# The mixer's output projection in seven block products, in an fp32 encoder kernel on one Trainium2 core

## The chip, the cores and the metric

The kernel runs on one core of one Trainium2 chip. The metric is the device time of one execution in microseconds (us), as the median of three runs.

## The reference

A trunk of two layers over x of 512 tokens by 1024 channels, in float32. Each layer is a half-step SwiGLU FFN, a token mixer, and another half-step FFN; one RMSNorm ends it. What the change touches is the last line of the mixer.

```python
def token_mixer(h, w_in, ..., w_out, lam_init):
    proj = h @ w_in
    ...
    gates = jax.nn.sigmoid(...)
    merged = gates[:, :, 0] * y_pool + gates[:, :, 1] * y_attn + gates[:, :, 2] * y_lru
    return merged @ w_out            # (512 x 1024) @ (1024 x 1024)

def reference(x, ...):
    for l in range(DEPTH):           # 2
        x = x + 0.5 * swiglu(rms_norm(x, ffn1_norm[l]), ffn1_w_in[l], ffn1_w_out[l])
        x = x + token_mixer(rms_norm(x, mix_norm[l]), ...)
        x = x + 0.5 * swiglu(rms_norm(x, ffn2_norm[l]), ffn2_w_in[l], ffn2_w_out[l])
    return rms_norm(x, final_norm)
```

## The kernel before

**Precision.** Every large matmul is done as three: each fp32 operand is split into a high part (a copy to a rounded type, on ScalarE, ACT) and a low part (operand minus high part, on VectorE, DVE), and hi·hi + hi·lo + lo·hi go into the same accumulator. For weights the parts are named `wh` and `wl`, for the merged activations `mg` (both parts), for the FFN's input `zh` and `zl`.

**Units.** The work is a list of units. A unit is a weight block of 128x1024 in SBUF (512 KB, tile `raw`, loaded by SyncE's queue, SP), its split, and its matmuls (`mm`). The main loop records a unit's matmuls and then a "gap" (`gap`), in which the work that stands between two units is recorded: the evictions of the unit just done (`after`), tasks that were deferred by so many gaps (`defer`), and the splits of the units up to `look` ahead (3 as a rule, up to 7 around a change of stage). Each engine then works through its own instructions in that order.

**Seven products.** The FFNs' two projections already use Strassen-Winograd's form (`seven`): rows and columns of the product and the contraction are each halved, and seven block products P1, P2, Q5, Q3, P6, P7, Q4 stand in for eight. Their left operands are blocks A11, A12, A22 of the activations or sums of them (S1 to S4). Their right operands are sums of weight blocks, and these are made by DMA: a block is loaded into `raw`, and when it has been split, GpSimd (POOL) issues a second DMA that accumulates the next block into the same tile. The results are added into the residual `x` (eight tiles of 128x512) by DVE, a product at a time (`put`, `total`); a product that is used more than once is first copied out of PSUM by ACT (tile `u`).

**The mixer's end.** Four units `y1` multiply the attention output by its branch weights, each for a pair of column chunks. After each, DVE merges the branches into tiles `gt` and splits them into `mg` (six ops of 128x512). Then the output projection: for each of two column halves four units of `w_out`, each with two contraction chunks for all four row tiles, into four PSUM banks `o`. At the end of a half DVE adds 0.5·`o` into `x`. Calls of `done` follow: ACT squares `x` for the norm, TensorE transposes it (`zt`), ACT evicts the transposes (`zf`), and `zh`, `zl` and sums `zs` are made for the FFN behind. In all but the last part of the projection the FFN's weights are split ahead.

Of the kernel before, what the change touches and what calls it, by code (L numbers as in the profile page):

```python
# [17 lines left out]
S = 512  # L18
# [89 lines left out]
def trunk_kernel(ctx, tc, xn, pm, fin, cst, bd, f1i, f1o, win, wbp, wba, wbl, wout, f2i, f2o, out):  # L108
# [72 lines left out]
    units = []  # L181
    hooks = {}
# [227 lines left out]
    LEFT = {"P1": "A11", "P2": "A12", "Q5": "S1", "Q3": "S4", "P6": "S2", "P7": "S3", "Q4": "A22"}  # L410

    def seven(order, nk, width, left, wap, after, held, prep=None, fresh=False):
# [6 lines left out]
        for p in order:  # L419
            name = LEFT[p]  # L420
            for n, (k0, k1) in enumerate(parts):
# [40 lines left out]
                units.append(Unit(block, flat((k1 - k0) * width), mm, fin, acc=acc, held=held[p] if isinstance(held, dict) else held, nk=k1 - k0))  # L462


    def ffn(wi, wo, done, order0, rf, lim0=12, wait=1):
# [176 lines left out]
        def prep(p, n, i):  # L642
            if n % 2 == 0:
                sums, parts = combos(LEFT[p], n // 2)
                if LEFT[p] in ("S1", "S4", "S3"):
                    add_hook(i - 4, sums)
                add_hook(i - 3, parts)
            else:
                add_hook(i, lambda k=(LEFT[p], n // 2): comb.pop(k))

        def put(hh, kk, src, sign=1.0):
            for tt in range(2):
                xv = x[2 * (hh ^ rf) + tt, kk]
                V.scalar_tensor_tensor(out=xv, in0=src[tt], scalar=0.25 * sign, in1=xv, op0=MUL, op1=ADD)

        def copies(dst):
            def fn(ps):
                dst.update(enumerate(two("u")))
                for tt in range(2):
                    A.activation(out=dst[tt], in_=ps[tt], func=AF.Copy)  # L660
            return fn

        def total(ps):
            for tt in range(2):
                V.tensor_tensor(out=u[tt], in0=ps[tt], in1=u[tt], op=ADD)

        def o_p1(ps):
            copies(u)(ps)
            later.append(lambda: put(0, 0, u))

        def o_p2(ps):
            later.append(lambda: put(0, 0, ps))
            defer(1, lambda: done(0 ^ rf, 0))

        def o_q5(ps):
            copies(q5)(ps)
            later.append(lambda: put(0, 1, q5))
            defer(1, lambda: later.append(lambda: put(1, 1, q5)))
            defer(2, q5.clear)

        def o_q3(ps):
            later.append(lambda: put(0, 1, ps))

        def o_p6(ps):
            later.append(lambda: (total(ps), put(0, 1, u, -1.0)))
            defer(1, lambda: done(0 ^ rf, 1))

        def o_p7(ps):
            later.append(lambda: (total(ps), put(1, 1, u, -1.0)))
            defer(1, lambda: (later.append(lambda: (put(1, 0, u), u.clear())), done(1 ^ rf, 1)))  # L690

        def o_q4(ps):
            put(1, 0, ps)
            done(1 ^ rf, 0)
# [5 lines left out]
        def left(name, k):  # L700
# [3 lines left out]
              {"P1": o_p1, "P2": o_p2, "Q5": o_q5, "Q3": o_q3, "P6": o_p6, "P7": o_p7, "Q4": o_q4},  # L704
# [3 lines left out]
    def mixer(l, side, done, between):  # L708
# [393 lines left out]
        def y1(cpair):  # L1102
# [83 lines left out]
        for ch in (1, 0):  # L1186
            box = {"held": []}
            for u4 in range(4):
                b = Block([load_fn(wout[l][u4 * 256:u4 * 256 + 256, ch * S:(ch + 1) * S].rearrange("(k p) f -> p k f", p=128), 2, S)])

                def part(ts, box):
                    for t in ts:
                        for k0, uh, ul in box["held"]:
                            for k in (k0, k0 + 1):
                                wh, wl = (a[:, (k - k0) * S:(k - k0 + 1) * S] for a in (uh, ul))
                                th, tl = (a[:, t * 128:(t + 1) * 128] for a in st["mg"][k])
                                PE.matmul(box["ps"][t], lhsT=th, rhs=wh, start=k == 0, stop=False)
                                PE.matmul(box["ps"][t], lhsT=th, rhs=wl, start=False, stop=False)
                                PE.matmul(box["ps"][t], lhsT=tl, rhs=wh, start=False, stop=k == KD - 1)

                def mm(u, a0, a1, u4=u4, ch=ch, box=box):
                    if u4 == 0:
                        box["ps"] = [bank("o") for _ in range(4)]
                    box["held"].append((2 * u4, u.hi, u.lo))
                    if ch == 0 and u4 >= 2:
                        if u4 == 3:
                            part((2, 3), box)
                        return
                    part(range(4), box)
                    box["held"].clear()  # L1210
# [409 lines left out]
```

## Time and profile before

| | |
|---|---|
| median of 3 runs | 2115.81 us (2114.51 to 2118.64) |
| the profiled execution's own time | 2117.74 us |
| its span, first to last instruction | 2115.9 us |
| mean granted TensorE clock | 0.997 |
| busy: TensorE / DVE / ACT / POOL | 2072.8 / 1658.6 / 1191.2 / 343.7 us |
| DMA | 314.61 MB, 149 GB/s |

Busy times are sums over the span. A matmul's row is longer than the distance to the next one, because matmuls are pipelined; what one costs is read from the starts of its neighbours. A number in square brackets behind an instruction in the timeline is the time for which its engine stood idle ahead of it, with what ended that. Almost every line reads L83, because a helper records the operations; the tile names tell them apart.

### The profile page before, as it was taken

How to read it: one execution, taken by the hardware profiler on the slowest of the kernel's cores; microseconds unless marked ns; L12 is line 12 of the kernel's file. 1: busy time of each engine (PE TensorE's matmuls, PEld its weight loads, DVE VectorE, ACT ScalarE, POOL GpSimd, SP SyncE). 2: the span in 40 equal slices, each digit the busy share in tenths (PEclk: the TensorE clock that was granted, in tenths of full speed). 3: DMA queues.
4: the chain of work that ended last, by engine and by line, in shares of the span. 5: the costliest groups of instructions: out<-in, count | busy, mean ns of one | idle time of the engine just before them, and what ended most of it. 6: DMA issues, size and time to landing. Idle time of an engine off the chain costs nothing.

```text
span 2115.9 us, 26228 instructions
## 1 busy us (share of the span) xinstructions
PE 2072.8 (98%) x9646; PEld 1734.1 (82%) x9646; DVE 1658.6 (78%) x2362; ACT 1191.2 (56%) x1766; POOL 343.7 (16%) x292
## 2 busy tenths in 40 slices
PE   8999999999999999999999999999999999999998
PEld 6988888788787889888879887887887877988786
DVE  6788898597677588779977878986967766788797
ACT  7555566645663565556755555665456536555564
POOL 1312230000000022213213222300000001322230
PEclk9999999999999999999999999999999999999999
DMA  9987997022226379889959879940221364887994
GB/s 252 180 184 159 210 193 216 1 79 90 70 80 189 80 148 193 162 203 196 228 104 205 172 157 239 183 154 20 84 82 54 117 180 79 163 192 164 205 179 102
DMA packets 194096, 314.61 MB, mean 149 GB/s; under 512 B 10544, under 2 KB 86832, under 8 KB 193968
## 3 DMA queue, kind: packets, MB, share of 16 engines
q0 software_dynamic: 76288, 138.43, 39.5%
q1 hardware_dynamic: 117392, 174.30, 24.8%
q8 instruction: 75, 1.23, 0.2%
q14 instruction: 53, 0.43, 0.1%
q10 hardware_dynamic: 288, 0.21, 0.0%
HBM read 310.80 MB, written 2.10 MB: 148 GB/s over the span
## 4 chain that ended last, share of the span: by engine, by line
PE 80%; DVE 9%; ACT 4%; DMA 4%; issue 2%; POOL 1%; DVEq 0%; SPq 0%; POOLq 0%; ACTq 0%
PE P L83 26%; PE Q L83 19%; PE ps L83 18%; PE o L83 4%; PE y L83 4%; DVE wl L83 4%; DMA raw<-in_f1i_dram 2%; PE v L83 2%; PE ht L83 2%; PE sc L83 1%; PE av L83 1%; ACT wh L83 1%; ACT zh L83 1%; DVE c L83 1%; DVE x L83 1%
## 5 line engine op out<-in xcount | busy, mean ns | idle before, releaser
L83 DVE TENSOR_TENSOR wl<-raw,wh 128x1024 fp32r<-128x1024 f32 (+2 forms) x696 | 705.7, 1038 | 163.4 <-ACT wh L83 153.7
L83 ACT ACTIVATE wh<-raw 128x1024 fp32r<-128x1024 f32 (+2 forms) x695 | 606.9, 906 | 208.2 <-DMA raw<-in_f2i_dram 53.0
L83 PE MATMUL ps<-z,wh 128*128 128x512 f32 x1216 | 380.1, 393 | 0.2
L372 POOL DMA_DIRECT2D raw<-in_f2i_dram x96 | 116.0, 1240 | 1114.4 <-DVE mg L83 353.2
L83 PE MATMUL P<-wl,zh 128*128 128x512 f32 (+1 forms) x768 | 287.3, 374 | 7.2 <-DVE wl L83 7.1
L83 PE MATMUL P<-wh,zh 128*128 128x512 f32 (+1 forms) x768 | 288.7, 376 | 4.7 <-ACT wh L83 3.1
L83 PE MATMUL P<-wh,zl 128*128 128x512 f32 (+1 forms) x768 | 286.5, 373 | 0.5 <-DVE zl L83 0.5
L83 PEld LDWEIGHTS ps<-z,wh 128*128 128x128 f32 x1216 | 227.1, 188 | 51.1 <-issue 3.4
L83 PE MATMUL ps<-z,wl 128*128 128x512 f32 x608 | 237.0, 390 | 0.0
L83 PE MATMUL Q<-wl,zh 128*128 128x512 f32 (+1 forms) x576 | 214.6, 373 | 6.1 <-DVE wl L83 6.1
L83 PE MATMUL Q<-wh,zh 128*128 128x512 f32 (+1 forms) x576 | 216.7, 376 | 2.1 <-ACT zh L83 1.9
L83 PE MATMUL Q<-wh,zl 128*128 128x512 f32 (+1 forms) x576 | 214.2, 372 | 1.0 <-DVE zl L83 1.0
L372 POOL DMA_DIRECT2D raw<-in_f1i_dram x96 | 116.1, 1236 | 366.9 <-DVE wl L83 274.2
L83 PEld LDWEIGHTS P<-wl,zh 128*128 128x128 f32 x768 | 145.1, 189 | 30.5 <-DVE wl L83 10.4
L83 PEld LDWEIGHTS P<-wh,zh 128*128 128x128 f32 x768 | 144.8, 189 | 25.7 <-ACT wh L83 3.5
L83 PEld LDWEIGHTS P<-wh,zl 128*128 128x128 f32 x768 | 145.0, 189 | 21.3 <-DVE zl L83 1.0
L83 PE MATMUL P<-wl,ah 128*128 128x512 f32 x352 | 138.1, 392 | 2.4 <-DVE wl L83 2.3
L83 PE MATMUL P<-wh,ah 128*128 128x512 f32 x352 | 137.5, 391 | 0.0
L83 PE MATMUL P<-wh,al 128*128 128x512 f32 x352 | 137.2, 390 | 0.0
L83 PEld LDWEIGHTS ps<-z,wl 128*128 128x128 f32 x608 | 114.1, 188 | 23.7
L83 PEld LDWEIGHTS Q<-wl,zh 128*128 128x128 f32 x576 | 108.2, 188 | 23.1 <-DVE wl L83 9.2
L83 PEld LDWEIGHTS Q<-wh,zh 128*128 128x128 f32 x576 | 108.2, 188 | 17.3 <-ACT zh L83 2.7
(192 smaller groups left out, 3414.4 us busy)
## 6 DMA issues: line engine op xcount, KB each, us to landing
raw<-in_win_dram SPq DMA_DIRECT2D x84, 512.0 KB, 4.7
raw<-in_f1i_dram POOLq DMA_DIRECT2D x64, 512.0 KB, 6.9
raw<-in_f2i_dram POOLq DMA_DIRECT2D x64, 512.0 KB, 6.9
raw<-in_f2i_dram SPq DMA_DIRECT2D x52, 512.0 KB, 5.5
raw<-in_f1i_dram SPq DMA_DIRECT2D x50, 512.0 KB, 6.2
raw<-in_f1o_dram POOLq DMA_DIRECT2D x40, 512.0 KB, 7.9
raw<-in_f2o_dram POOLq DMA_DIRECT2D x40, 512.0 KB, 8.3
raw<-in_f1o_dram SPq DMA_DIRECT2D x30, 512.0 KB, 7.5
```

The lines of the kernel that those rows point to most:

```text
L83: return fn(*args, **kw)
L372: return lambda raw: GP.dma_start(out=raw[:, 0:n * w].rearrange("p (k f) -> p k f", f=w), in_=src, accum_op=ADD)
```

## The change

The output projection of the mixer goes through `seven` as the FFNs do, in the order P1, P2, Q5, P7, P6, Q3, Q4, so that A11 and A12 come first. The merged tiles `gt` are kept (`st["mf"]`), sums S1 to S4 of them are made in DVE (`ms`), and split into `mh` and `ml`. What the FFN's output projection does with its results moves into a function, `added`, that both use. The start of the projection joins the list of places around which units are split further ahead (up to seven).

```diff
-    LEFT = {"P1": "A11", "P2": "A12", "Q5": "S1", "Q3": "S4", "P6": "S2", "P7": "S3", "Q4": "A22"}
+    SEVEN = {"P1": "A11", "P2": "A12", "Q5": "S1", "Q3": "S4", "P6": "S2", "P7": "S3", "Q4": "A22"}
...
                 elif p == "Q3":
                     block = b2[n] = Block([ld(1, 1)])
-                    acc = ap(0, 1)
+                    acc = ap(0, 1) if order.index("P7") > order.index("Q3") else None
+                elif order.index("P7") < order.index("Q3"):
+                    block = Block([ld(1, 1)], ap(0, 1))
...
+    def added(scale, rf, done, seventh=False):
...
+        def put(hh, kk, src, sign=1.0):
+            for tt in range(2):
+                xv = x[2 * (hh ^ rf) + tt, kk]
+                V.scalar_tensor_tensor(out=xv, in0=src[tt], scalar=scale * sign, in1=xv, op0=MUL, op1=ADD)
...
+        def p1(ps):
+            copies(u)(ps)
+            later.append(lambda: put(0, 0, u))
+            if seventh:
+                defer(1, lambda: later.append(lambda: put(0, 1, u, -1.0)))
+
+        def p2(ps):
+            later.append(lambda: put(0, 0, ps))
+            defer(1, lambda: done(0 ^ rf, 0))
+
+        def q5_(ps):
+            copies(q5)(ps)
+            later.append(lambda: put(0, 1, q5))
+            defer(1, lambda: later.append(lambda: put(1, 1, q5)))
+            defer(2, q5.clear)
+
+        def q3(ps):
+            if seventh:
+                put(0, 1, ps)
+                return done(0 ^ rf, 1)
...
+        def p6(ps):
+            if seventh:
+                later.append(lambda: (total(ps), put(1, 1, u, -1.0), put(0, 1, ps, -1.0)))
+                return close22()
...
+        def p7(ps):
+            if seventh:
+                return later.append(lambda: total(ps))
...
+        def close22():
+            defer(1, lambda: (later.append(lambda: (put(1, 0, u), u.clear())), done(1 ^ rf, 1)))
+
+        def q4(ps):
+            put(1, 0, ps)
+            done(1 ^ rf, 0)
...
+                if cpair == 3:
+                    defer(1, lambda: m_sum("S1"))
+                    defer(2, lambda: m_sum("S3"))
+                    defer(4, lambda: m_sum("S2"))
+                    defer(6, lambda: m_sum("S4"))
...
-        for ch in (1, 0):
-            box = {"held": []}
-            for u4 in range(4):
...
-                def part(ts, box):
...
+        def m_sum(name):
+            a, b, op = {"S1": ("A21", "A22", SUB), "S2": ("S1", "A11", SUB), "S3": ("A11", "A21", SUB), "S4": ("A12", "S2", ADD)}[name]
+            a, b = m_block(a), m_block(b)
+            t = sums[name] = big(name="ms")
+            for o, p, q in zip(m_block(name), a, b):
+                V.tensor_tensor(out=o, in0=p, in1=q, op=op)
+            hi, lo = big(F32R, "mh"), big(F32R, "ml")
+            A.activation(out=hi, in_=t, func=AF.Copy)
+            later.append(lambda: V.tensor_tensor(out=lo, in0=t, in1=f(hi), op=SUB))
+            mc[name] = (hi, lo)
...
+        results = added(0.5, rf, done, True)
+        changes.append(len(units))
...
+        seven(["P1", "P2", "Q5", "P7", "P6", "Q3", "Q4"], 4, S, left, wap, {p: then(p) for p in results}, 12)
...
-                units[i - 6 + k].look = look
+                units[i - 6 + k].look = max(look, units[i - 6 + k].look)
```

The next rows are DVE's in the changed kernel, in the middle of the projection of layer 0, from the row behind the low part of S1 to the second update of `x_116`. `x_114` and `x_116` are the tiles that the first transposes read, `ms_5813` is S1, `ms_5835` S3 and `ms_5887` S2; `u_5832` is the copy of P1's results, `P2_5860` a PSUM bank of P2, `gt` the merged tiles.

```order
L83 TENSOR_TENSOR ms_5835<-gt_3981 128x512
L83 TENSOR_TENSOR ms_5835<-gt_5066 128x512
L83 SCALAR_TENSOR_TENSOR x_114<-u_5832,x_114 128x512
L83 SCALAR_TENSOR_TENSOR x_116<-u_5832,x_116 128x512
L83 TENSOR_TENSOR ml_5839<-ms_5835,mh_5838 128x1024
L83 TENSOR_TENSOR wl_5842<-raw_5599,wh_5841 128x1024
L83 SCALAR_TENSOR_TENSOR x_118<-u_5832,x_118 128x512
L83 SCALAR_TENSOR_TENSOR x_120<-u_5832,x_120 128x512
L83 TENSOR_TENSOR ms_5887<-ms_5813,gt_3981 128x512
L83 TENSOR_TENSOR ms_5887<-ms_5813,gt_5066 128x512
L83 SCALAR_TENSOR_TENSOR x_114<-P2_5859,x_114 128x512
L83 SCALAR_TENSOR_TENSOR x_116<-P2_5860,x_116 128x512
```

In the kernel before DVE's rows at that place, from the last `mg` of layer 0 to the first half's evictions, are these.

```order
L83 TENSOR_TENSOR mg_5766<-gt_5540,mg_5766 128x512
L83 TENSOR_TENSOR wl_5769<-raw_5513,wh_5768 128x1024
L83 TENSOR_TENSOR wl_5806<-raw_5556,wh_5805 128x1024
L83 TENSOR_TENSOR wl_5843<-raw_5589,wh_5842 128x1024
L83 TENSOR_TENSOR wl_5873<-raw_5663,wh_5872 128x1024
L83 SCALAR_TENSOR_TENSOR x_118<-o_5779,x_118 128x512
L83 SCALAR_TENSOR_TENSOR x_120<-o_5780,x_120 128x512
L83 SCALAR_TENSOR_TENSOR x_98<-o_5777,x_98 128x512
L83 SCALAR_TENSOR_TENSOR x_100<-o_5778,x_100 128x512
```

Four splits and four evictions stood there; now twelve ops stand between S1's low part and the tiles that the first transposes read.

TensorE's rows at the place where these transposes now stand, between the last matmuls of Q5 and the first of P7 (`cst` holds the identity).

```order
L83 MATMUL Q5_5902<-wl_5750,mh_5816 128x512
L83 MATMUL Q5_5902<-wh_5749,ml_5817 128x512
L83 MATMUL zt_5942<-cst_71,x_114 128x128
L83 MATMUL zt_5942<-cst_71,x_116 128x128
L83 MATMUL zt_5942<-cst_71,x_114 128x128
L83 MATMUL zt_5942<-cst_71,x_116 128x128
L83 MATMUL zt_5949<-cst_71,x_114 128x128
L83 MATMUL zt_5949<-cst_71,x_116 128x128
L83 MATMUL zt_5949<-cst_71,x_114 128x128
L83 MATMUL zt_5949<-cst_71,x_116 128x128
L83 MATMUL P7_5964<-wh_5790,mh_5838 128x512
```

Before, the first transposes stood between matmuls of the second column half and read `x` tiles whose evictions were the last DVE work of the first half. Now they stand between two products, and the second of them reads the last row of the DVE piece above.

The third place is the transposes in the middle of Q4. On DVE, the last rows up to the tiles that they read are these in the changed kernel (`Q3_6056` and `Q3_6057` are Q3's banks, `raw_5711` and `raw_5796` already weights of the next FFN).

```order
L83 SCALAR_TENSOR_TENSOR x_118<-P6_6000,x_118 128x512
L83 SCALAR_TENSOR_TENSOR x_120<-P6_6001,x_120 128x512
L83 TENSOR_TENSOR wl_6039<-raw_5473,wh_6038 128x1024
L83 TENSOR_TENSOR wl_6042<-raw_5708,wh_6041 128x1024
L83 SCALAR_TENSOR_TENSOR x_106<-u_5832,x_106 128x512
L83 SCALAR_TENSOR_TENSOR x_108<-u_5832,x_108 128x512
L83 TENSOR_TENSOR wl_6076<-raw_5711,wh_6075 128x1024
L83 TENSOR_TENSOR wl_6079<-raw_5796,wh_6078 128x1024
L83 SCALAR_TENSOR_TENSOR x_118<-Q3_6056,x_118 128x512
L83 SCALAR_TENSOR_TENSOR x_120<-Q3_6057,x_120 128x512
```

The updates from Q3 stand behind three splits of the next FFN's weights. In the kernel before, at the end of its second half, DVE's rows ahead of the last evictions but two were these.

```order
L83 TENSOR_TENSOR wl_6020<-raw_5732,wh_6019 128x1024
L83 TENSOR_TENSOR wl_6023<-raw_5774,wh_6022 128x1024
L83 TENSOR_TENSOR wl_6032<-raw_5809,wh_6031 128x1024
L83 TENSOR_TENSOR wl_6035<-raw_5812,wh_6034 128x1024
L83 SCALAR_TENSOR_TENSOR x_114<-o_5930,x_114 128x512
L83 SCALAR_TENSOR_TENSOR x_116<-o_5931,x_116 128x512
```

What moved: the splits ahead of the next FFN stood there before too, but ahead of one addition to each `x` tile; now each tile is updated up to five times in the stage.

## Rows read from the trace of the kernel before

**Rows 1.** The page's first part: busy us, share of the span, instructions.

```profile
PE 2072.8 (98%) x9646; PEld 1734.1 (82%) x9646; DVE 1658.6 (78%) x2362; ACT 1191.2 (56%) x1766; POOL 343.7 (16%) x292
```

**Rows 2.** Waits of TensorE by releaser: us in total, times, longest.

```profile
PE P L83 <- DVE wl L83: 9.4, 10, 1.7
PE Q L83 <- DVE wl L83: 7.6, 12, 2.1
```

**Rows 3.** Timeline of TensorE, layer 0: start, us, instruction, count.

```profile
667.63 0.39 PE L83 MATMUL y<-at,wl 128*128 128x512 f32 x1
...
680.80 0.39 PE L83 MATMUL o<-wh,mg 128*128 128x512 f32 x1
...
681.26 0.61 PE L83 MATMUL o<-wh,mg 128*128 128x512 f32 x2
...
681.94 0.61 PE L83 MATMUL o<-wh,mg 128*128 128x512 f32 x2
```

**Rows 4.** Stretches of 20 us: busy us of each engine, clock, DMA share, GB/s.

```profile
660.00:680.00 20.00, 18.89 (x81) 14.71 (x80) 16.54 (x25) 6.74 (x10) 2.41 (x2) 1.00 0.65 175
680.00:700.00 20.00, 20.00 (x90) 16.57 (x89) 11.60 (x14) 6.64 (x8) 0.00 (x0) 1.00 0.63 185
700.00:720.00 20.00, 20.00 (x99) 16.78 (x98) 12.29 (x13) 13.28 (x24) 2.42 (x2) 1.00 0.16 43
720.00:740.00 20.00, 18.67 (x89) 14.99 (x88) 12.47 (x26) 12.04 (x25) 1.23 (x2) 1.00 0.53 98
```

**Rows 5.** Timeline of DVE, layer 0, the mixer's end.

```profile
666.55 0.69 DVE L83 TENSOR_TENSOR at<-o,at 128x512 fp32r<-128x512 f32 x1 [0.69 <-ACT at L83]
...
669.77 0.68 DVE L83 SCALAR_TENSOR_TENSOR gt<-gt,y 128x512 f32<-128x512 f32 x1
...
673.81 0.68 DVE L83 SCALAR_TENSOR_TENSOR gt<-gt,y 128x512 f32<-128x512 f32 x1
...
687.87 4.63 DVE L83 TENSOR_TENSOR wl<-raw,wh 128x1024 fp32r<-128x1024 f32 x4 [0.26 <-ACT wh L83]
...
702.76 1.89 DVE L83 SCALAR_TENSOR_TENSOR x<-o,x 128x512 f32<-128x512 f32 x3 [0.67 <-PE o L83]
...
720.85 0.69 DVE L83 SCALAR_TENSOR_TENSOR x<-o,x 128x512 f32<-128x512 f32 x1 [0.70 <-PE o L83]
```

**Rows 6.** Timeline of ACT, layer 0, the same place.

```profile
686.79 3.89 ACT L83 ACTIVATE wh<-raw 128x1024 fp32r<-128x1024 f32 x4
...
708.64 3.03 ACT L83 ACTIVATE zf<-zt,par 128x256 f32<-128x256 f32 x8 [1.30 <-PE zt L83]
...
722.73 0.20 ACT L83 ACTIVATE m<-m 128x2 f32<-128x2 f32 x1 [0.43 <-DVE m L83]
```

**Rows 7.** DMA issues from 640 to 800 us: count, KB, median us to landing.

```profile
raw<-in_f2i_dram POOLq DMA_DIRECT2D x8, 512.0 KB, 7.0
```

**Rows 8.** Timeline of TensorE at the FFN's Q5, layer 0 and layer 1.

```profile
734.32 0.50 PE L83 MATMUL Q<-wh,zh 128*128 128x512 f32 x1 [0.81 <-ACT zh L83]
...
735.58 0.50 PE L83 MATMUL Q<-wh,zl 128*128 128x512 f32 x1 [0.52 <-DVE zl L83]
...
1780.67 0.50 PE L83 MATMUL Q<-wh,zl 128*128 128x512 f32 x1 [0.53 <-DVE zl L83]
```

**Rows 9.** The page's part on DMA issues, the slowest group there.

```profile
raw<-in_f2o_dram POOLq DMA_DIRECT2D x40, 512.0 KB, 8.3
```

**Rows 10.** Timeline of TensorE between the layers.

```profile
1068.12 0.33 PE L83 MATMUL zt<-cst,x 128*128 128x128 f32 x1 [2.88 <-DVE x L83]
...
1080.39 0.54 PE L83 MATMUL P<-wh,zl 128*128 128x512 f32 x1 [0.53 <-DVE zl L83]
1080.73 0.63 PE L83 MATMUL P<-wh,zh 128*128 128x512 f32 x1
...
1084.14 0.39 PE L83 MATMUL P<-wh,zl 128*128 128x512 f32 x1
```

**Rows 11.** One stretch there, columns as in rows 4.

```profile
1082.00:1083.00 1.00, 1.00 (x4) 0.80 (x3) 0.61 (x1) 0.36 (x1) 0.97 (x1) 0.50 0.00 0
```

More of the change, by code (lines that the diff above doesn't have):

```diff
@@ L462, in seven, with copies, fn, total @@
                 units.append(Unit(block, flat((k1 - k0) * width), mm, fin, acc=acc, held=held[p] if isinstance(held, dict) else held, nk=k1 - k0))
+    def added(scale, rf, done, seventh=False):
+        u, q5 = {}, {}
+        def put(hh, kk, src, sign=1.0):
+            for tt in range(2):
+                xv = x[2 * (hh ^ rf) + tt, kk]
+                V.scalar_tensor_tensor(out=xv, in0=src[tt], scalar=scale * sign, in1=xv, op0=MUL, op1=ADD)
+        def copies(dst):
+            def fn(ps):
+                dst.update(enumerate(two("u")))
+                for tt in range(2):
+                    A.activation(out=dst[tt], in_=ps[tt], func=AF.Copy)
+            return fn
+        def total(ps):
+            for tt in range(2):
+                V.tensor_tensor(out=u[tt], in0=ps[tt], in1=u[tt], op=ADD)
+        def p1(ps):
[15 more added lines that the diff above has]
+                return done(0 ^ rf, 1)
+            later.append(lambda: put(0, 1, ps))
+        def p6(ps):
+            if seventh:
+                later.append(lambda: (total(ps), put(1, 1, u, -1.0), put(0, 1, ps, -1.0)))
+                return close22()
+            later.append(lambda: (total(ps), put(0, 1, u, -1.0)))
+            defer(1, lambda: done(0 ^ rf, 1))
+        def p7(ps):
+            if seventh:
+                return later.append(lambda: total(ps))
+            later.append(lambda: (total(ps), put(1, 1, u, -1.0)))
+            close22()
+        def close22():
[3 more added lines that the diff above has]
+            done(1 ^ rf, 0)
+        return {"P1": p1, "P2": p2, "Q5": q5_, "Q3": q3, "P6": p6, "P7": p7, "Q4": q4}
     def ffn(wi, wo, done, order0, rf, lim0=12, wait=1):
@@ L648, in prep @@
             else:
[L649 to L694, printed above, removed]
+                add_hook(i, lambda k=(SEVEN[p], n // 2): comb.pop(k))
+        results = added(0.25, rf, done)
         def wap(r, c, k0, k1):
@@ L1185, in mixer @@
         units[n0].between = between
-        for ch in (1, 0):
-            box = {"held": []}
-            for u4 in range(4):
-                b = Block([load_fn(wout[l][u4 * 256:u4 * 256 + 256, ch * S:(ch + 1) * S].rearrange("(k p) f -> p k f", p=128), 2, S)])
-                def part(ts, box):
[L1192 to L1210, printed above, removed]
-                def evict(hh, ch, box):
-                    for tt in range(2):
-                        t = 2 * hh + tt
-                        V.scalar_tensor_tensor(out=x[t, ch], in0=box["ps"][t], scalar=0.5, in1=x[t, ch], op0=MUL, op1=ADD)
-                    done(hh, ch)
-                def after(u4=u4, ch=ch, box=box):
-                    if u4 == 3:
-                        evict(1, ch, box)
-                        if ch == 1:
-                            evict(0, ch, box)
-                            box.clear()
-                units.append(Unit(b, flat(), mm, after, held=11))
@@ L1227, in last_mm, with m_block @@
-        def last_mm(u, a0, a1, box=box):
-            part((0, 1), box)
-            box["held"].clear()
-            st["mg"] = None
-        def last_after(box=box):
-            evict(0, 0, box)
-            box.clear()
-        units.append(Unit(None, [], last_mm, last_after, held=11))
+        rf = 1
+        sums = {}
+        def m_block(name):
+            if name in sums:
+                return [sums[name][:, j * S:(j + 1) * S].rearrange("p (c q) -> p c q", c=2) for j in range(2)]
+            r, k = (int(name[1]) - 1) ^ rf, int(name[2]) - 1
+            return [t.rearrange("p (c q) -> p c q", c=2)[:, :, r * 256:r * 256 + 256] for j in range(2) for t in (st["mf"][2 * k + j],)]
```

38 lines of the change are left out of this document (31 added, 7 removed).

## The prediction

> **What bounds the kernel now.** I read the page's first part first: TensorE is busy for 98% of the span, VectorE (DVE) for 78%, ScalarE (ACT) for 56% [rows 1]. Time follows TensorE, and the question for an edit is how much matmul it removes and how many waits it adds. The list of TensorE's waits comes next: 17 us for weight splits `wl` in the whole kernel [rows 2]. Then the stage itself: in the output projection of layer 0 the 128x512 matmuls follow each other without a gap, three of them (hi·hi, hi·lo, lo·hi) in 681.94 - 681.26 = 0.68 us (two start in the first of these rows, one between them), so 0.2267 us each; the stage starts at 680.80 [rows 3]. Last I read DVE in stretches of 20 us from 660 to 740: 16.5, 11.6, 12.3 and 12.5 us busy [rows 4], so it has 27 us free in these 80, most of it inside the projection. That free time is what the change spends.
>
> **What the change removes.** Eight block products (two row halves, two column halves, two halves of the contraction) become seven. One is 2 row tiles x 4 chunks x 3 = 24 matmuls, so there are 48 fewer in the two layers: 5.44 us a layer at 0.2267 us, 10.9 us in all, if TensorE stays gapless.
>
> **What it adds.** Per layer DVE gets six more weight splits `wl` (14 units in place of 8) and four low parts `ml`, ten ops of 128x1024; and eight adds `ms` and 24 updates and totals in place of 8 evictions, 24 more ops of 128x512. A `wl` follows the one ahead of it after 1.13 us (four in 4.63 us, the last 1.23 us long); a 512 op follows an independent one after 0.60 us (three in 1.89 us), and one on which it depends after 0.72 us [rows 5]. I take 1.135 and 0.63. That makes 10 x 1.135 + 24 x 0.63 = 26.5 us more DVE work, against 5.44 us less on TensorE. The 27 us free above would just hold it if each could be used where it stands.
>
> It can't. From P1 to Q4 a product takes TensorE 5.44 us, and DVE on average 2.57 ops of 1024 and 4.57 of 512, 5.8 us; and DVE enters the stage with the merges of the last two column pairs still to do. The stage turns from TensorE's into DVE's. ACT gets six `wh`, four `mh` and four copies, some 12 us, and has more than that free [rows 4], but each stands between two DVE ops. SP issues six loads in place of eight, GpSimd eight accumulating DMAs; DMA is busy for 0.63 of the time in the first 20 us of the stage and 0.16 in the second [rows 4], so I cost the bytes at nothing, and only the landing of one accumulate below.
>
> **The walk**, in the clock of the trace of before, layer 0. DVE is free after the last attention low part, at 667.24 [rows 5]; the first merge tile is complete on TensorE at 667.63 + 0.39 = 668.02 [rows 3]. The merge of one pair of column chunks takes DVE 673.81 - 669.77 = 4.04 us [rows 5]. In the new order two pairs come first (to 676.1), then four `wl`, the last behind ACT's fourth copy (0.95 us apart, four in 3.89 us [rows 6]), to 681.0, then the third pair to 685.1. TensorE reaches P1 at 680.80 as before and finds all it needs.
>
> Next on ACT is the copy for the second half of Q5, whose weights are an accumulating DMA that can be issued when `wl` of P1's second half ends, at 677.7. The nearest row for its landing is 7.0 us [rows 7]: about 685. Behind that copy stand, on ACT and DVE, the fourth pair's `mg`. So `wl` ends near 687.4 and the fourth pair at 691.5; P2's second half wants it from 689, and TensorE waits some 1.5 us. Then come `wl`, the two adds of S1, ACT's `mh` (1.05 us) and `ml`, at 696.55: Q5 waits 2.1 us for `mh` and 0.8 for `ml`, and ends at 701.6 in place of 697.1. From 696.5 DVE has ten 512 ops and two of 1024 before `x` is complete for the first transposes, 10 x 0.63 + 2 x 1.135 = 8.6 us: 705.1. **TensorE waits 3.5 us there.**
>
> P7, P6, Q3 and half of Q4 (84 matmuls) with 16 transposes run on to 725.8. DVE has 18 ops of 512 and 11 of 1024 in that stretch, 11.3 + 12.5 us, and 1.4 us of holes while ACT is held by evictions of the transposes (eight in 3.03 us [rows 6]): the two updates from Q3 end at 730.3, and the transposes that need them stand in the middle of Q4. **TensorE waits 4.5 us.** After the rest of Q4 (733.8) the next FFN's first matmul needs its `zh`. From an update's end to the end of ACT's small root it took 722.93 - 721.54 = 1.4 us [rows 5, 6]; four evictions, two `wh` and the `zh` follow on ACT, 1.5 + 1.9 + 1.05 us: 736.1, a wait of 2.3 us, and `zl` holds it 1.1 us more. The next transposes wait 1.0 us for `x`, and the third matmul of the FFN's Q5, which needs `zl` of S1, comes at 745.7. In the trace of before it comes at 735.58, after waits of 0.81 and 0.52 us [rows 8]. Layer 0 ends up **10.1 us late**: 16.8 us of waits, less the 1.3 that stood there, less the 5.4 saved. From there DVE has the work of before and some four units of split weights in hand, so I let the delay stay and not grow.
>
> Layer 1 has the same seam (1780.67 [rows 8]) and the same order on DVE, op for op: 10.1 us again. The sum is +20.2 us on the profiled execution's own 2117.74 us, 2138. That execution lies 1.9 us above the median of the runs shown, so I forecast **2136 us**.
>
> **Bounds.** With all 512 ops at 0.60, or all at 0.72 us, the 28 of them between 696.5 and 730.3 move a layer by -1 or +2.5 us. If the accumulate of Q5's second half landed at once, DVE would gain 1.9 us a layer; at 8.3 us, the slowest median on the page [rows 9], it loses 1.3. The holes behind ACT, 1.2 us at S1 and 1.4 at P6, could close. All good ends: 5 us a layer less, 2126. All bad ends: 4 us more, 2144.
>
> **The rivals.** (a) The clock. In the trace of before TensorE waited 2.88 us, ran on, waited 0.53 us more some 12 us later, and then issued eight matmuls 0.427 us apart in place of 0.2267 before it came back; the granted clock there is 0.50, the level of 1.2 GHz [rows 10, 11]. That cost 8 x 0.2 = 1.6 us. The new order has four waits of about two us or more in each layer. A half clock between two waits for DVE costs nothing, since TensorE only waits less; behind the last wait it is paid, once or twice a layer, 3 to 6 us in all: 2139 to 2142. The Trainium skill, TensorE: Matmul & The Clock Gate, HAM oscillation, says that idle gaps between groups of matmuls put the array back to half clock, and that this is paid again at every gap. By that rule the time would be the 2142 just worked out. The long wait in [rows 10] was not followed by a half clock at once: 0.15.
>
> (b) Faster. The place is the first transposes behind Q5: if DVE completes `x` before 697.1, when gapless matmuls would leave Q5, it has no queue, nothing on the seam waits long, and the change gives its 10.9 us less a little: 2106. DVE's 40% of free time in the stage speaks for it [rows 4]; against it, that at this point it would have to be 8 us ahead of the walk, more than all its holes up to there. 0.12.
>
> (c) About the same. The queue is real, but half of the delay is won back in the FFN behind, where waits for `wl` vanish as the splits stand further ahead of a late TensorE: 2112 to 2120. Against it, [rows 2] has only 17 us of such waits in the whole kernel. 0.10.
>
> (d) The accumulates chain: the weights of Q5, P6 and Q4 each wait for the split of the same buffer, and a late one holds ACT and all that is behind it. Two stalls of 3 us a layer that the walk doesn't have give 12 us more: 2148. Nothing in [rows 7] asks for them. 0.08.
>
> **How the numbers follow.** The forecast, 2126 to 2144, has 0.55. The range 2119 to 2150 takes in (a), (d) and the upper end of (c), about 0.8. A measurement of this kernel tells a change of about 0.2% (4.2 us) from none. Faster is (b), 0.12; within 0.2% is most of (c), 0.09; slower is the rest, 0.79.
>
> **What would show it.** In the profile after: DVE above 90% busy from 685 to 735; TensorE waiting for `x` at the transposes behind Q5 and inside Q4, 3 to 5 us each (`zt` at some 18 us more in the list of waits), for `mh` and `ml` at Q5 (2 to 3 us), and for `zh` ahead of the FFN (2 us); the third matmul of the FFN's Q5 near 746. If the transposes wait under 1 us each, (b) is right and the forecast wrong; if matmuls behind the seam run at a granted clock of 0.50, (a); if DVE has long holes because ACT waits for `raw` of `wout`, (d).

## The result, and the profile after

The changed kernel takes 2132.02 us (median of four runs, 2131.14 to 2133.03) where the kernel before takes 2115.16 us beside it: 1.0080 of its time, interval 1.0068 to 1.0092. It is 16.9 us slower; 20 us slower was forecast. The profiled execution has a span of 2130.6 us, 14.7 us more than before. The first part of its page, and the head of the list of TensorE's waits (us in total, times, longest), stand against [rows 1, 2]:

```profile
PE 2071.9 (97%) x9598; PEld 1730.1 (81%) x9598; DVE 1709.6 (80%) x2430; ACT 1213.6 (57%) x1794; POOL 363.0 (17%) x308
```

```profile
PE zt L83 <- DVE x L83: 14.5, 11, 3.0
PE P L83 <- DVE wl L83: 8.8, 10, 1.7
PE Q L83 <- DVE wl L83: 6.3, 10, 2.2
PE Q L83 <- ACT mh L83: 3.9, 2, 2.0
...
PE P L83 <- ACT zh L83: 2.4, 2, 2.0
```

The waits for weight splits are nearly what they were (15.1 us in place of 17.0). New are transposes that wait for `x`, and products that wait for `mh` and `zh`. TensorE's timeline of layer 0 shows them in their order, from the first of the last attention products `y` to the third matmul of the FFN's Q5 (that one was at 735.58 before, and `y` at 666.57); the last two rows are of layer 1, the transposes in the middle of Q4 and the same matmul of Q5:

```profile
665.76 0.51 PE L83 MATMUL y<-at,wh 128*128 128x512 f32 x1 [0.88 <-ACT at L83]
...
689.27 0.73 PE L83 MATMUL P<-wh,mg 128*128 128x512 f32 x2 [0.50 <-DVE mg L83]
...
694.00 0.50 PE L83 MATMUL Q<-wh,mh 128*128 128x512 f32 x1 [1.98 <-ACT mh L83]
...
695.25 0.51 PE L83 MATMUL Q<-wh,ml 128*128 128x512 f32 x1 [0.52 <-DVE ml L83]
...
703.02 0.33 PE L83 MATMUL zt<-cst,x 128*128 128x128 f32 x1 [2.47 <-DVE x L83]
...
704.64 0.78 PE L83 MATMUL P<-wh,mh 128*128 128x512 f32 x1
...
728.27 0.33 PE L83 MATMUL zt<-cst,x 128*128 128x128 f32 x1 [2.07 <-DVE x L83]
...
734.56 0.63 PE L83 MATMUL P<-wh,zh 128*128 128x512 f32 x1 [1.98 <-ACT zh L83]
...
736.21 0.80 PE L83 MATMUL P<-wh,zl 128*128 128x512 f32 x1 [0.59 <-DVE zl L83]
736.80 0.63 PE L83 MATMUL P<-wh,zh 128*128 128x512 f32 x1
737.23 0.63 PE L83 MATMUL P<-wl,zh 128*128 128x512 f32 x1
...
745.18 0.39 PE L83 MATMUL Q<-wh,zl 128*128 128x512 f32 x1
...
1780.79 0.33 PE L83 MATMUL zt<-cst,x 128*128 128x128 f32 x1 [2.97 <-DVE x L83]
...
1796.59 0.50 PE L83 MATMUL Q<-wh,zl 128*128 128x512 f32 x1 [0.42 <-DVE zl L83]
```

From `y` to that matmul, the **stretch** in what follows, layer 0 now takes 745.18 - 665.76 = 79.4 us; before it took 735.58 - 666.57 = 69.0. In layer 1 it is 79.3 against 69.3. So each layer loses 10.4 and 10.0 us here, and that is the whole loss between the two profiled executions: 20.4 us, of which 4.9 are won back behind the two places, and 0.8 ahead of the first.

The stretch as one row for each layer, two rows of before and then two of after (length, then busy us of TensorE, its weight loads, DVE, ACT and GpSimd with their instructions, granted clock, DMA share, GB/s), and three more rows of after:

```profile
666.57:735.58 69.01, 67.45 (x311) 55.38 (x311) 45.74 (x67) 33.96 (x60) 6.05 (x5) 1.00 0.50 130
1711.41:1780.67 69.26, 67.45 (x310) 55.38 (x310) 45.76 (x67) 34.07 (x60) 6.05 (x5) 1.00 0.50 130
```

```profile
665.76:745.18 79.42, 68.55 (x287) 53.74 (x287) 69.12 (x99) 43.84 (x73) 10.86 (x9) 0.94 0.64 154
1717.32:1796.59 79.27, 68.03 (x286) 52.75 (x287) 68.00 (x98) 42.76 (x70) 10.86 (x9) 0.96 0.65 155
685.00:735.00 50.00, 39.95 (x173) 30.87 (x171) 43.80 (x62) 28.32 (x47) 8.07 (x7) 0.96 0.75 185
704.50:707.50 3.00, 3.00 (x10) 2.42 (x9) 3.00 (x5) 2.51 (x7) 0.95 (x1) 0.50 0.02 5
1783.00:1786.00 3.00, 3.00 (x8) 2.30 (x7) 1.35 (x5) 3.00 (x7) 0.00 (x0) 0.50 0.90 156
```

DVE's work in the stretch rose from 45.7 to 69.1 us. TensorE with the waits of before would need about 69.0 - 5.4 = 63.6, so DVE now has more to do than TensorE. The row from 704.50 to 707.50, and the 0.427 us from 736.80 to 737.23 in the timeline, show a second cost: in layer 0, behind the waits of 2.47 and 1.98 us (the latter at 734.56), TensorE runs on at a granted clock of 0.50, the level of 1.2 GHz, for some seven matmuls the first time, and for twelve and the transposes behind them the second. Behind the 1.98 us at 694.00 and the 2.07 at 728.27 it does not. In layer 1 it does so behind the first transposes again, and behind the wait of 2.97 us in Q4 (the last row above), not ahead of the FFN.

### The profile page after: what moved, and what is told of

Same layout as the page of the kernel before. It is cut to its first block, busy times and chain, and to the rows that moved or that the text cites. A ratio compares the mean times of both kernels' runs of the same rounds, so it can differ in the third digit from the quotient of the medians.

```text
span 2130.6 us, 26295 instructions
## 1 busy us (share of the span) xinstructions
PE 2071.9 (97%) x9598; PEld 1730.1 (81%) x9598; DVE 1709.6 (80%) x2430; ACT 1213.6 (57%) x1794; POOL 363.0 (17%) x308
## 4 chain that ended last, share of the span: by engine, by line
PE 77%; DVE 9%; issue 6%; ACT 4%; DMA 3%; POOL 1%; SPq 0%; DVEq 0%; POOLq 0%; ACTq 0%
PE P L83 28%; PE Q L83 20%; PE ps L83 18%; DVE wl L83 4%; PE y L83 3%; PE v L83 2%; PE ht L83 2%; PE sc L83 1%; DMA raw<-in_wout_dram 1%; POOL raw L373 1%; PE av L83 1%; ACT wh L83 1%; DMA raw<-in_f2i_dram 1%; DVE x L83 1%; DVE al L83 1%
## 5 line engine op out<-in xcount | busy, mean ns | idle before, releaser
L83 DVE TENSOR_TENSOR wl<-raw,wh 128x1024 fp32r<-128x1024 f32 (+2 forms) x708 | 719.7, 1041 | 155.2 <-ACT wh L83 144.4
L83 ACT ACTIVATE wh<-raw 128x1024 fp32r<-128x1024 f32 (+2 forms) x707 | 618.9, 909 | 221.7 <-DMA raw<-in_f2i_dram 49.8
L83 PEld LDWEIGHTS P<-wl,zh 128*128 128x128 f32 x768 | 145.4, 189 | 30.5 <-DVE wl L83 10.4
L83 PEld LDWEIGHTS P<-wh,zh 128*128 128x128 f32 x768 | 145.4, 189 | 27.8 <-ACT zh L83 4.2
L373 POOL DMA_DIRECT2D raw<-in_wout_dram x16 | 19.2, 1203 | 762.1 <-DVE gt L83 660.9
```

The lines of the kernel that those rows point to most:

```text
L83: return fn(*args, **kw)
L373: return lambda raw: GP.dma_start(out=raw[:, 0:n * w].rearrange("p (k f) -> p k f", f=w), in_=src, accum_op=ADD)
```

## The experiments

Each ran beside the kernel before; all ratios are to that. Its median was from 2112.4 to 2115.2 us in the different rounds, and an interval is some 0.0015, or 3 us, to either side: small differences between two runs' medians say little, and the text sets runs against each other by their ratios and stretches. The stretches are read as above, from `y` to the third matmul of Q5, in layer 0 and layer 1 of the profiled execution.

| run | median us | before beside it | ratio (interval) | stretches us |
|---|---|---|---|---|
| the change | 2132.0 | 2115.2 | 1.0080 (1.0068 to 1.0092) | 79.4, 79.3 |
| 1 no updates from `u`, `q5` | 2130.1 | 2114.8 | 1.0078 (1.0063 to 1.0093) | 76.4, 76.4 |
| 2 two matmuls of three | 2131.6 | 2114.8 | 1.0082 (1.0067 to 1.0097) | 78.1, 77.8 |
| 3 plain loads | 2130.6 | 2114.8 | 1.0077 (1.0062 to 1.0092) | 78.9, 77.5 |
| 4 sums on GpSimd | 2142.4 | 2114.8 | 1.0134 (1.0117 to 1.0151) | 83.1, 82.9 |
| 5 = 1 and 3 | 2118.6 | 2112.4 | 1.0031 (1.0022 to 1.0041) | 73.7, 73.7 |
| 6 no longer look | 2137.5 | 2112.4 | 1.0114 (1.0098 to 1.0129) | 81.9, 81.8 |
| 7 P7 second | 2127.2 | 2112.4 | 1.0065 (1.0050 to 1.0080) | 76.5, 76.5 |
| 8 = 7, half splits | 2127.1 | 2112.4 | 1.0066 (1.0049 to 1.0083) | 75.8, 75.8 |
| 9 = 8, late splits | 2127.1 | 2115.2 | 1.0060 (1.0045 to 1.0075) | 75.2, 74.8 |
| 10 = 9, early splits | 2126.8 | 2115.2 | 1.0060 (1.0043 to 1.0076) | 72.6, 72.5 |
| 11 before, DVE loaded | 2137.9 | 2115.2 | 1.0113 (1.0098 to 1.0128) | 80.5, 80.5 |
| 12 = 8, 1 and 3 | 2117.0 | 2113.5 | 1.0015 (1.0006 to 1.0024) | 72.3, 71.2 |

**1. DVE with less to do.**

```diff
         def put(hh, kk, src, sign=1.0):
+            if seventh and (src is u or src is q5):
+                return
```

> The changed kernel without the twelve updates of x a layer that read the copies u and q5 (left out of the computation); matmuls, weight loads, splits, copies and the updates from PSUM stay. Theory (DVE's queue sets the seam): 12 x 0.63 = 7.6 us of DVE work a layer less, 2.5 of it ahead of the first transposes and 5.0 ahead of those in Q4, so both waits for x (2.47 and 2.07 us) and most of the wait for zh (1.98) go, those for mg, mh and ml ahead of them stay: 7 to 9 us a layer at the seam, of which the FFN behind gives part back, 2116 to 2122. Rival (the accumulating loads and ACT's copies set the waits): the waits stay and the time is 2128 to 2132.

The median fell by 2.0 us, which the ratios do not tell from none; it missed the theory's range by 8 and lies in the rival's. The stretches are 3.1 and 2.9 us shorter, which is more than the median shows: this profiled execution came to its first stretch 2.6 us later than the changed kernel's, over instructions that are the same in both (it waited 0.57 and 0.77 us for `wl` near 250 us). The wait at the first transposes is gone but for 0.27 us; the one in Q4 is not. DVE's work in the stretch fell from 69.1 to 61.1 us, but much of that became idle time: the updates from Q3 end 61.1 us behind `y`, in place of 63.0. ACT's rows and DVE's of this run, layer 0:

```profile
721.66 2.01 ACT L83 ACTIVATE wh<-raw 128x1024 fp32r<-128x1024 f32 x2 [4.66 <-DMA raw<-in_wout_dram]
```

```profile
722.75 2.36 DVE L83 TENSOR_TENSOR wl<-raw,wh 128x1024 fp32r<-128x1024 f32 x2 [2.10 <-ACT wh L83]
...
728.15 1.28 DVE L83 SCALAR_TENSOR_TENSOR x<-Q,x 128x512 f32<-128x512 f32 x2
```

ACT waits 4.66 us for an accumulate to land, DVE 2.10 us for ACT, and the transposes behind the updates from Q3 wait 2.97 us. In the changed kernel ACT's row at this place reads:

```profile
720.68 2.01 ACT L83 ACTIVATE wh<-raw 128x1024 fp32r<-128x1024 f32 x2 [4.98 <-DMA raw<-in_wout_dram]
```

The accumulate is as late there, but DVE has other work and stands idle for only 0.52 us. This suggests two chains that end nearly together; run 5 puts it to the test.

**2. TensorE with less to do.** In `seven`, for the projection alone:

```diff
-                            PE.matmul(acc_, lhsT=ah, rhs=wl, start=False, stop=False)
-                            PE.matmul(acc_, lhsT=al, rhs=wh, start=False, stop=k == nk - 1)
+                            PE.matmul(acc_, lhsT=ah, rhs=wl, start=False, stop=short and k == nk - 1)
+                            if not short:
+                                PE.matmul(acc_, lhsT=al, rhs=wh, start=False, stop=k == nk - 1)
```

> The changed kernel without the third matmul of each triple in the projection (the product of the low part of the activations is left out of the computation): 56 matmuls a layer less, 12.7 us of TensorE a layer at 0.2267, all other engines' work as it was. Theory (the stage is DVE's from P2 to the next FFN): TensorE waits longer at the same places and the end of the stage hardly moves, 2124 to 2132. Rival (TensorE and its clock set the stage, the waits being a small part): 25 us less, about 2107.

25.4 us of matmuls are gone and 0.4 us of time; the stretches are 1.3 and 1.5 us shorter. The waits of transposes for `x` rose from 14.5 to 22.9 us, one of them to 5.1, and the granted clock in layer 0's stretch fell from 0.94 to 0.85. TensorE's work does not bound the stage.

**3. Without accumulates.** Each weight block a `load` of its own in place of `load` and `acc`.

```diff
+                if direct:
+                    r_, c_ = {"P1": (0, 0), "P2": (1, 0), "Q5": (1, 1), "P7": (1, 1), "P6": (1, 0), "Q3": (1, 1), "Q4": (0, 0)}[p]
+                    block, acc = Block([ld(r_, c_)]), None
```

> The changed kernel with a plain load for each of the projection's 14 weight blocks in place of six loads and eight accumulating DMAs (the sums of weight blocks are left out of the computation). Theory: only the short holes go in which DVE waits for ACT's copy of a late block, 0.3 us ahead of P2 and 1.2 at P6: 2128 to 2132. Rival (each accumulate waits for the split of the same buffer, and its landing holds ACT and DVE): 3 to 6 us a layer faster, 2120 to 2126.

1.4 us in the median: inside the theory's range, and not told from none. The stretches are 0.5 and 1.8 us shorter. Alone, the accumulates cost little.

**4. The sums S1 to S4 on GpSimd.**

```diff
-                V.tensor_tensor(out=o, in0=p, in1=q, op=op)
+                GP.tensor_tensor(out=o, in0=p, in1=q, op=op)
```

> The changed kernel with the eight sums ms a layer on GpSimd in place of DVE, same result. Theory: 8 x 0.63 = 5.0 us of DVE work a layer goes to an engine that is 83% idle; if an add there takes less than about 1.3 us, the waits for mh, for x behind Q5 and for x in Q4 fall by about 1, 2 and 2 us: 2118 to 2126. Rival: GpSimd is slow (over 2 us an add) or holds DVE up, S1 comes later than before, and the time is 2130 to 2140.

The rival, and more: 10.4 us slower than the change. GpSimd's adds take from 1.5 to 2.3 us, and beside them most of DVE's rows with two SBUF operands take far longer. Timeline of DVE, then of GpSimd:

```profile
687.53 0.68 DVE L83 SCALAR_TENSOR_TENSOR gt<-gt,y 128x512 f32<-128x512 f32 x1
688.25 2.73 DVE L83 TENSOR_TENSOR gt<-gt 128x512 f32<-128x512 f32 x1
...
693.20 2.30 DVE L83 TENSOR_TENSOR wl<-raw,wh 128x1024 fp32r<-128x1024 f32 x1
```

```profile
688.15 2.26 POOL L1234 TENSOR_TENSOR ms<-gt 128x512 f32<-128x512 f32 x1
691.05 5.58 POOL L1234 TENSOR_TENSOR ms<-gt 128x512 f32<-128x512 f32 x3 [0.64 <-DVE gt L83]
```

An add of 128x512 beside GpSimd's takes 2.73 us in place of 0.69, a split 2.30 in place of 1.22. The trace shows a second cost: GpSimd's two adds for S4 stand behind the issue of an accumulating DMA and start at 709.88, ACT then waits 4.97 us for them, and DVE 4.33 us for ACT (at 713.99). How the 10.4 us divide between the two was not tested.

**5. Both chains at once** (the diffs of 1 and 3).

> Both of the first and the third run at once: no updates from u and q5, and plain loads in place of accumulates (updates and sums of weight blocks are left out of the computation). Alone they gave 2.0 and 1.4 us. Theory (two chains end nearly together, DVE's queue and, through ACT, the accumulates of Q5, P6 and Q4): together they give far more than the sum, both waits for x go, and the time is 2114 to 2122. Rival (a third thing sets the seam, the sums S1 and the tail from x to zh): about the sum, 2126 to 2130.

Inside the theory's range. By the ratios it is 0.49%, or 10.4 us, better than the change (13.4 us in the medians, but the kernel before was 2.7 us faster in this round). In the stretches it gains 5.7 us in layer 0 and 5.5 in layer 1, where runs 1 and 3 alone gave 3.1 + 0.5 and 2.9 + 1.8: the two are worth 2.1 and 0.9 us more together than apart, and not four times as much, as the medians' 13.4 against 3.4 would have it. The waits of transposes for `x` show the two chains best (us in total, times, longest; runs 1, 3 and 5):

```profile
PE zt L83 <- DVE x L83: 9.9, 7, 3.0
PE zt L83 <- DVE x L83: 11.0, 8, 3.1
PE zt L83 <- DVE x L83: 3.3, 3, 2.9
```

Either alone leaves waits of 1.5 to 3.1 us in Q4. With both out no transpose of the two stretches waits over 0.2 us; the 2.9 is the wait between the layers that stood there before [rows 10]. Both chains are real, and at the transposes in Q4 each alone was in part hidden behind the other.

**6. The look ahead undone.**

```diff
         results = added(0.5, rf, done, True)
-        changes.append(len(units))
```

> The changed kernel without the start of the projection in the list of places around which units are split further ahead; same result. Theory (DVE's total work in the stage counts, the order little): splits stand later, the waits for mg and x get shorter and waits for wl take their place, 2126 to 2134. Rival (the splits ahead of the updates are what costs): 4 units a layer leave the queue ahead of the transposes, 2118 to 2124.

5.5 us slower than the change in the medians, 7 by the ratios, and outside both ranges. The splits now come too late: P2 waits 1.43 us for `wh` and 0.75 for `wl`, P6 1.17 and 0.76, and the transposes in Q4 still wait 3.81 us. Splitting further ahead is what this change needs, not what it pays for.

**7. P7 second.** S3 reads only the first two pairs of the merge.

```diff
+                if cpair == 2:
+                    defer(0, lambda: m_sum("S3"))
                 if cpair == 3:
-                    defer(1, lambda: m_sum("S1"))
-                    defer(2, lambda: m_sum("S3"))
+                    defer(2, lambda: m_sum("S1"))
...
-        seven(["P1", "P2", "Q5", "P7", "P6", "Q3", "Q4"], 4, ...
+        seven(["P1", "P7", "P2", "Q5", "P6", "Q3", "Q4"], 4, ...
```

> The changed kernel with the products in the order P1, P7, P2, Q5, P6, Q3, Q4, and S3 made right behind the third pair's merge (S3 reads only the first two pairs, so P7 can start early); same result and the same work on every engine. Theory: TensorE has 5.4 us of work more ahead of P2, so the waits for mg, mh and ml (3 us with what they cost behind them 3.5) go and the first wait for x shrinks by some 2 us; the later ones stay, since DVE's sum is the same: 4 us a layer, 2122 to 2127. Rival (DVE's sum alone counts): the waits move to Q4, 2129 to 2134.

4.8 us faster than the change in the medians, just outside the theory's range; by the ratios 3 us, with intervals that overlap. The stretches are 3.0 and 2.8 us shorter. The waits for `mg`, `mh` and `ml` are gone but for 0.51 us; a part of them came back as waits of transposes for `x` (18.1 us in the whole run in place of 14.5).

**8. Half splits, 9. late splits, 10. early splits**, one on top of the other (`starts` are the projections' first units, `ends` the next FFNs'; run 8 has the first piece alone; run 9 has `usual` around `starts`, and not the two lines on `held`):

```diff
+                    if c < 4:
+                        hi, lo = pair(F32R, "mg")
+                        A.activation(out=hi[:, S // 2:], in_=t[:, S // 2:], func=AF.Copy)
...
+        for u in units[-8:]:
+            u.held = max(u.held, 12)
...
-        changes.append(len(units))
+        starts.append(len(units))
...
-        changes.append(len(units))
+        ends.append(len(units))
...
-    for i in changes:
-        for k, look in enumerate((4, 5, 6, 7, 7, 7, 6, 6, 5, 5, 4, 4)):
+    usual = (4, 5, 6, 7, 7, 7, 6, 6, 5, 5, 4, 4)
+    for i, table in [(i, usual) for i in changes] + [(i, (8, 8, 8, 7, 7, 7, 6, 6, 5, 5, 4, 4)) for i in starts] + [(i, (3, 3, 4, 4, 6, 7, 6, 6, 5, 5, 4, 4)) for i in ends]:
+        for k, look in enumerate(table):
```

> As the run before, and the merged tiles of the first two pairs are split only in the row half that a product reads (A21 is no left operand); same result. 4 x 0.27 us less DVE and 4 x 0.2 us less ACT work a layer, where DVE's queue is longest. Theory: 1 to 2 us faster than the run before in all, 2120 to 2126. Rival: no difference.

> The eighth run's kernel with units split less far ahead just before the next FFN (3, 3, 4, 4 in place of 4, 5, 6, 7 for P6 and Q3); same result. DVE's updates from Q3 then stand behind three splits instead of four or five and come 2.3 us earlier. Theory (DVE's queue up to the update from Q3 sets the wait of 3.0 us in Q4): that wait shrinks to about 1 us, the splits come behind it while TensorE has work: 2 us a layer, 2121 to 2125. Rival (the splits are wanted at once by the next FFN): waits for wl take its place, 2126 to 2130.

> As the run before, and the first splits of the output projection's weights are made further ahead (8 units in place of 4 and 5 ahead of the last gates, with 12 blocks loaded ahead in place of 8), so that four of the projection's first splits are done ahead of the attention's last head, where DVE is busy for 14 us of 26; same result. Theory: 3 x 1.135 = 3.4 us less DVE work a layer behind that point: 2114 to 2121. Rival (the splits delay the attention's end, or the later waits don't hang on the work ahead of them): 2122 to 2130.

Three times the rival by the number: neither median nor ratio moved beyond the noise. In 9 the second wait in Q4 went as forecast (a row of `zt` at 724.68 waits 0.27), but waits for `zh` (1.04) and for the next `x` (1.26) took part of its place, and 0.6 us of layer 0's stretch is all that was left; no wait for `wl` came up there, which the rival had named as the reason. In 10 the stretch got 2.6 us shorter, but it started 4.2 us later, at 670.15 in place of 665.99, and 3.7 of these came up behind 650 us, where the splits had moved ahead of the attention's end. TensorE's timeline of this run there:

```profile
663.86 1.13 PE L83 MATMUL nrm<-o,cst 128*128 128x512 f32 x2 [1.94 <-ACT o L83]
...
670.15 0.49 PE L83 MATMUL y<-at,wh 128*128 128x512 f32 x1 [1.06 <-ACT at L83]
```

**11. The kernel before, with DVE loaded**, behind each unit of the projection (and four more adds at the end):

```diff
+        def load(n):
+            for _ in range(n):
+                V.tensor_tensor(out=slot(name="idle"), in0=cs[:, C_DIST:C_DIST + S], in1=cs[:, C_DIST + 128:C_DIST + 128 + S], op=ADD)
...
                 def after(u4=u4, ch=ch, box=box):
+                    load(5)
...
         def last_after(box=box):
+            load(4)
```

> The kernel before with 44 adds of 128x512 a layer on DVE that nothing reads, five behind each unit of the output projection (four behind the last), 44 x 0.60 = 26.4 us, as much as the change was reckoned to add; TensorE keeps its eight products. Theory (DVE's load makes the stage DVE's): DVE has 45.7 + 26.4 = 72 us of work in a stretch that lasts 69.0, so the stretch grows by 3 to 8 us a layer, 2119 to 2128. Rival (the load fits into DVE's free time, and it is the chains of the new products that cost): 2112 to 2117.

22.8 us slower than before, more than the theory's 13 and outside both ranges. Nothing of the seven products is in this kernel, and yet it waits for the same tiles, for `x` and then for `zh`. Two rows of its timeline and its stretch:

```profile
730.54 2.26 PE L83 MATMUL zt<-cst,x 128*128 128x128 f32 x8 [4.46 <-DVE x L83]
...
745.62 0.50 PE L83 MATMUL Q<-wh,zh 128*128 128x512 f32 x1 [3.64 <-ACT zh L83]
```

```profile
666.41:746.88 80.47, 71.02 (x310) 57.44 (x310) 71.82 (x111) 33.51 (x60) 6.01 (x5) 0.96 0.43 112
```

**12. Everything out at once** (7, the half splits, 1 and 3).

> The eighth run's kernel (order P1, P7, P2, ..., half of the first four merged tiles split) without the updates from u and q5 and with plain loads in place of the accumulates (both left out of the computation, as in the fifth run): all three causes gone at once. Theory: DVE's work of the stage falls below TensorE's 63.6 us, the waits for mh, ml and mg of the fifth run (3.3 us a layer) go as well, and the saved matmuls show at last: 2106 to 2113, faster than the kernel before. Rival (the tail, from the last update of x to zh, and the half clock behind each wait hold the stage whatever DVE does): 2115 to 2119.

The rival: 2117.0 us, and still not below the kernel before. DVE is down to 60.6 us of work in layer 0's stretch, less than TensorE's 63.6, and the saving still does not show. The transposes behind Q5 still wait 1.84 and 0.27 us, those in Q4 0.69 and 0.27, and the tail, from the last updates to `zh` and `zl`, costs two waits more. TensorE's rows at the start of the FFN:

```profile
727.79 0.70 PE L83 MATMUL P<-wh,zh 128*128 128x512 f32 x1 [1.97 <-ACT zh L83]
...
729.44 0.80 PE L83 MATMUL P<-wh,zl 128*128 128x512 f32 x1 [0.52 <-DVE zl L83]
730.03 0.63 PE L83 MATMUL P<-wh,zh 128*128 128x512 f32 x1
730.46 0.63 PE L83 MATMUL P<-wl,zh 128*128 128x512 f32 x1
```

The updates from Q3 end at 722.04 in this run, and `zh` is there 5.8 us later; the rest of Q4 and eight transposes don't fill that. Behind the wait the matmuls again come 0.43 us apart. So a DVE with less work than TensorE is not enough; that the tail alone is what remains is not shown, since the first transposes wait too.

## Why the prediction was right, point by point

**The stage turns from TensorE's into DVE's: shown.** Run 2 takes 25 us from TensorE and the time moves by 0.4 us; run 11 gives the old kernel a like load on DVE and costs 22.8 us. The change's gross price is 16.9 + 10.9 = 27.8 us, so a load of this size can account for most of it; that the chains of the new products (S1, the accumulates) make up the rest is argued, not shown. The 26.5 us were a fair count: DVE's busy time in the stretch grew by 23.4.

**The walk on DVE: right within about 1.5 us.** The trace after runs 0.8 us ahead of the one before at `y`; with that taken off, the walk is within 0.7 us. DVE's rows of the changed kernel, layer 0:

```profile
675.69 4.63 DVE L83 TENSOR_TENSOR wl<-raw,wh 128x1024 fp32r<-128x1024 f32 x4 [0.26 <-ACT wh L83]
...
684.74 1.22 DVE L83 TENSOR_TENSOR wl<-raw,wh 128x1024 fp32r<-128x1024 f32 x1 [0.30 <-ACT wh L83]
...
689.39 0.69 DVE L83 TENSOR_TENSOR mg<-gt,mg 128x512 fp32r<-128x512 f32 x1 [0.17 <-ACT mg L83]
...
693.98 1.23 DVE L83 TENSOR_TENSOR ml<-ms,mh 128x1024 fp32r<-128x1024 f32 x1 [1.20 <-ACT mh L83]
...
702.28 1.28 DVE L83 SCALAR_TENSOR_TENSOR x<-P,x 128x512 f32<-128x512 f32 x2
...
721.78 2.36 DVE L83 TENSOR_TENSOR wl<-raw,wh 128x1024 fp32r<-128x1024 f32 x2 [0.52 <-ACT wh L83]
...
727.53 1.28 DVE L83 SCALAR_TENSOR_TENSOR x<-Q,x 128x512 f32<-128x512 f32 x2
```

The four `wl` end at 680.3 (forecast 681.0), the fourth pair at 690.1 (691.5), `ml` at 695.2 (696.6), the first transposes' tiles at 703.6 (705.1), Q3's updates at 728.8 (730.3). One item in it was wrong: the accumulate for Q5's second half did not hold the fourth pair, DVE stood idle for 0.30 us there, and P2 waited 0.50 in place of 1.5 us. (No `x` tile is updated more than four times in the stage, from P1, Q5, P6 and Q3; the five times named ahead of the prediction are one too many.)

**The loss of a layer, 10.1 us: measured 10.4 and 10.0. Its terms were off, and made up for each other,** so that the sum came out this close is in part luck. The idle times that the timeline of layer 0 names add up to 10.7 us where 16.8 were forecast: `mg` 0.5 (1.5), `mh` and `ml` 2.5 (2.9), the first transposes 2.5 and 0.3 (3.5), those in Q4 2.1 and 0.3 (4.5), `zh` and `zl` 2.6 (3.4), the transposes behind them none (1.0). What the walk left out is the half clock. Going over all rows of the stretch from one start to the next, less 0.2267 us for a matmul and 0.79 for eight transposes, 13.0 us of excess stand at rows with a wait and 5.7 elsewhere, mostly in matmuls 0.43 us apart and the transposes beside them; before it was 2.2 and 0.7. The difference, 15.8 us, less the 5.4 saved, is the 10.4.

The largest mis-sized term is the wait in Q4. Counted from `y`, TensorE came to it 1.2 us later than the walk has it, in both layers, because P7 had begun at half clock (the seven matmuls from 704.64 on), so it waited less; DVE's updates from Q3 ended 0.7 us earlier than in the walk in layer 0, and 0.3 later in layer 1, where the wait is 2.97 us. As rival (a) puts it, a half clock between two waits for DVE only shortens the second. Behind the last wait it is paid, and that is so in layer 0 alone (from 734.56 on, 2.9 us): in layer 1 it falls into the rest of Q4, ahead of a wait for `zh` that is 0.38 us there in place of 1.98. Rival (a) was thus present in both layers, for the most part in the place of waits and not on top of them. (In [rows 10] the half clock stands behind a third wait that the prediction doesn't name, 1.26 us for `zh` at 1079.13, as well as behind the 0.53.) The Trainium skill, TensorE: Matmul & The Clock Gate, HAM oscillation, tells of a kernel in which the waits between groups of matmuls brought the half clock back each time; its waits were longer than those here, and the prediction's wording, idle gaps of any length, is wider than that. Of layer 0's four waits of about two us the half clock stands behind two, and not behind the one at 694.00 nor behind that of 728.27.

**"I let the delay stay": wrong by 4.9 us.** The delay of 9.6 us at Q5 is 5.9 at the next layer's `y`: the waits for `wl` at 763.63 (0.74 us) and at 1286 and 1293 (0.45 and 0.82) are gone, as is one of 1.26 for `zh` between the layers, and two others of 0.34 and 0.55 are new. Behind layer 1 another 1.2 us is won back. That is a quarter of the 20.4 us, where rival (c) had half. How much of it is rival (c)'s mechanism stays open: executions that run the same instructions up to the first stretch reached it up to 2.6 us apart (run 1), with waits for `wl` at places of the same kind. With the forecast loss and this gift the forecast would have been 2131.

**Rival (b), DVE not late: refuted,** the first transposes wait 2.47 us. **Rival (d), the accumulates:** they were late (ACT waits 4.98 us), but covered by DVE's own queue; without the cover, in run 1, they take its place in part. The sum was safe against that; a forecast for a lighter DVE would not have been.

**The signs named ahead.** DVE above 90% from 685 to 735: 43.8 of 50 us, 88%. `zt` some 18 us up in the list of waits, 3 to 5 us each: 11.3 up, 2.1 to 3.0 each. `mh` and `ml` 2 to 3 us: 2.5. `zh` 2 us: 1.98 in layer 0, 0.4 in layer 1. Q5's third matmul near 746: 745.18. No long holes of DVE for `raw` of `wout`: one of 0.52 us.

Open: whether seven products can pay here at all. Of the versions that compute the same, the best is still 0.6% slower than before. What was not tried is to shorten the tail: ACT makes the `zh` that the FFN's first matmul needs behind the squares of the tiles from Q3, which wait for DVE.

## What to carry to other kernels

A product fewer on TensorE is paid for on the engine that splits and adds: count that engine's us in the same stretch, and if its new sum passes TensorE's (here 69 against 64), expect the saving to be gone; other orders of the same work won back a quarter of the loss here by the ratios. A sum below TensorE's is no promise either (run 12). When taking work from the late engine changes little, look for a second chain that ends just behind it, and take both away in one run before the theory is dropped. Read such runs in the stretch that was changed, too: a median over the whole kernel can carry 2 us from elsewhere. A wait in TensorE can cost the clock behind it as well as its length, but only what lies behind the last wait is paid.

## What the runs showed of the hardware that was not expected

An add on GpSimd holds DVE up rather than helping it (run 4): 128x512 adds on DVE went from 0.69 to 2.73 us, splits from 1.22 to 2.30, while GpSimd's took 1.5 to 2.3 us each. The Trainium skill, SBUF — State Buffer, Who interferes with whom, says that a DVE instruction with two SBUF inputs contends with a GpSimd instruction that reads SBUF. These rows have two SBUF inputs and agree. Whether a DVE row with one operand in PSUM is spared is not shown: `gt<-gt,y` kept its 0.68 us at 687.53, but ended as GpSimd's first add began, and no other such row ran beside one for longer than 0.14 us. And in layer 0 the half clock came behind a wait of 1.98 us at 734.56 and not behind one of 1.98 us at 694.00: the length of the wait alone does not tell it.
